# One tanh for each sigmoid, two logarithms for the forget gate, and powers on GpSimd in a two-layer hybrid trunk

## The chip, the core and the metric

The kernel runs on one core of a Trainium2 chip. A core has five engines that each work off a list of their own in order: TensorE (PE: matmuls, with PEld for its weight loads), VectorE (DVE), ScalarE (ACT: one activation function per element with a scale and a bias), GpSimd (POOL) and SyncE (SP: here it issues most of the DMAs). They meet through semaphores. The metric is device time in microseconds (us) of one execution; the time of a kernel is the median over its runs.

## The reference

A trunk of two layers works on x of 256 tokens by 2048 features. What each layer computes, cut to what matters here:

```python
hn = rms_norm(h, norm_w[l])
proj = hn @ w_in[l]                        # 2048 x 8208
# group A, DeltaNet: 8 heads of 128
qkv = silu(causal_conv(dn_qkv, conv_w))
q, k = l2_norm(q) * 128 ** -0.5, l2_norm(k)
beta, g = sigmoid(b), -exp(A_log) * softplus(a + dt_bias)
# group B, HGRN2: 8 heads of 128
q = silu(hg_q)
log_f = log(lb + (1 - lb) * sigmoid(f))    # then summed up over each chunk: G
k = (1 - lb) * sigmoid(-f)
# both: o = recurrence(...); o = rms(o) * norm_w * silu(z)
h = h + concat(y_a, y_b) @ w_out[l]
h = h + (p[l] @ w_ple_up[l]) * sigmoid(h @ w_ple_gate[l])
```

A last rms_norm with final_norm_w ends it. Everything is float32.

## The kernel before

TensorE's fast path for four-byte numbers rounds them, so each matrix is split in two parts, hi (the rounded copy) and lo (the rest), and a product is three matmuls: hi by hi, hi by lo, lo by hi. The weights are read in the order in which they are used, as weight steps of two row tiles of 128 by 512 columns. For each step SP loads `raw` (three buffers, L378), ACT copies it to `whi` (L400), DVE subtracts to `wlo` (L402), and PE does twelve matmuls (L336, in `products`): for each of two token halves and each of two row tiles one with whi, one with wlo, one with whi. A step is prepared up to two steps ahead (`LOOK`), in three buffers of whi and wlo.

Per layer three stages follow one another on PE: in (17 chunks of up to 512 columns of w_in, 16 row tiles each), out (four chunks of w_out) and gate (four chunks of w_ple_gate, with the small product with w_ple_up). The 17 chunks are ordered by hand (`in_order`): the DeltaNet columns k and q of the four groups of two heads, then columns f and q of the HGRN2 groups, mixed with the rest. Whenever a chunk is complete, its mixer starts beside the following chunks: DeltaNet in class `DN`, HGRN2 in class `HG`. A tile named hg11 belongs to HGRN2 in layer 1, group 1; dn03 is DeltaNet in layer 0, group 3. Each mixer is a generator that waits a number of weight steps (tables `DELAY` and `DELAY_AT`) between its parts.

The order of PE is the order of the code: each matmul is kept in program order. On ACT, DVE and POOL a scheduler, which places each instruction by its own estimate of when it can run, writes the order, so that a mixer's operations and the whi and wlo of coming steps are interleaved by that estimate. An engine never goes past an instruction that waits: a wlo that stands behind a gate operation waits for it.

What the change touches, by name:

- `sigmoid` (L461) makes 1/(1 + exp(-x)) from an Exp on ACT, a min and an add on DVE, a Ln and an Exp on ACT. It is used for the convolutions (`conv`), for `gate_z` (SiLU of z, with a product on POOL, L590), in `f_side` and in `q_side`.
- `f_side` of HG (L967 to 979) takes the columns f: e = exp(-f) bounded (L467, L468), sg = the sigmoid (L469 to 471), k = e * (1 - lb) * sg (L974, one instruction for each of the two heads), log f as Ln of (1 - lb) * sg + lb (L975), and G as a running sum over the tokens (L979). `q_side` then makes q (L991) and factors out of G (tiles X, L1012 and following), part by part.
- `after_gate` (L1169) and `Finish.gate` (L1203 to 1208) write the same sigmoid out by hand for the gate stage. `after_gate` serves all chunks but the last one of layer 1, `Finish` that one, in pieces of 256 columns, since nothing runs beside it.
- inverse roots are a Ln and an Exp with scale -0.5 (`rms_factor` L609 and L610; `invn` and `nq` in DN), in `rms_token` and `Finish.rt` with one Newton step behind (L540 to 544).
- `write_gates` (L1139 and following) makes beta and g of DeltaNet, with an Exp and a Ln; the change leaves its code alone.
- ACT holds the tables of a few functions at a time. Before loads one set that has both Exp and Ln, once at the start (L237).

Of the kernel before, what the change touches and what calls it, by code (L numbers as in the profile page):

```python
# [166 lines left out]
def trunk(ctx: ExitStack, tc: tile.TileContext, head, xT, x, pT, W, par, fw, cst, msk, eye, out):  # L167
# [59 lines left out]
    def first_loads():  # L227
# [9 lines left out]
        S.preload_act_table_set("natural_log_exp_and_others")  # L237
# [35 lines left out]
    epsc = cp.tile([128, 1], F32, name="epsc")  # L273
    G.memset(epsc, EPS)
    lnhd = cp.tile([128, 1], F32, name="lnhd")
    G.memset(lnhd, float(-0.5 * np.log(128.0)))
# [31 lines left out]
    oml = cp.tile([128, DEPTH, 8], F32, name="oml")  # L308

    def gate_constants():  # L310

        S.activation(negA, P("alog", 0, DEPTH * 16), AF.Exp)
# [16 lines left out]
        V.tensor_scalar(oml, lb, -1.0, 1.0, ALU.mult, ALU.add)  # L329

# [130 lines left out]
    def sigmoid(dst, src, e=None):  # L461

        if e is None:
            S.activation(dst, src, AF.Exp, scale=-1.0)
            V.tensor_scalar(dst, dst, BIG, 1.0, ALU.min, ALU.add)
        else:
            S.activation(e, src, AF.Exp, scale=-1.0)  # L467
            V.tensor_scalar(e, e, BIG, None, ALU.min)  # L468
            V.tensor_scalar(dst, e, 1.0, None, ALU.add)  # L469
        S.activation(dst, dst, AF.Ln)  # L470
        S.activation(dst, dst, AF.Exp, scale=-1.0)
# [67 lines left out]
    def rsqrt_newton(r, x, t):  # L539
        S.activation(r, x, AF.Ln)  # L540
        S.activation(r, r, AF.Exp, scale=-0.5)
        V.tensor_tensor(t, r, r, ALU.mult)
        V.scalar_tensor_tensor(t, t, -0.5, x, ALU.mult, ALU.mult)
        V.scalar_tensor_tensor(r, t, 1.5, r, ALU.add, ALU.mult)
        return r
# [37 lines left out]
    def gate_z(ps, c0, rt, name):  # L583
# [5 lines left out]
        sigmoid(sz, zs)  # L589
        G.tensor_tensor(sz, zs, sz, ALU.mult)  # L590
# [153 lines left out]
    class DN:  # L744
# [12 lines left out]
        def dz(self, ps, c0):  # L757
            self.sz = gate_z(ps, c0, self.row.rt, self.n)
            self.done.add("z")
            yield 1  # L760
# [24 lines left out]
        def conv(self, ps, which):  # L785
# [11 lines left out]
            sg = tmp(n + "sg")  # L797
            sigmoid(sg, ac)
            return ac, sg

        def conv_silu_kq(self, ps, which, w):
            ac, sg = self.conv(ps, which)
            for t in range(2):
                V.tensor_tensor(self.kq[t][:, :, w, :], v4(ac)[:, t::2], v4(sg)[:, t::2], ALU.mult)
# [24 lines left out]
        def k_side(self):  # L829
# [7 lines left out]
            lk = small("lk")  # L837
            S.activation(lk, ss, AF.Ln, bias=epsc)
            self.invn = small("invn", 4, NG + 1)
            S.activation(self.invn, lk, AF.Exp, scale=0.5)  # L840
# [7 lines left out]
        def q_side(self):  # L848
# [22 lines left out]
            lq = small("lq")  # L871
            S.activation(lq, ss, AF.Ln, bias=epsc)
            self.nq = small("nq", 4, NG + 1)
            S.activation(self.nq, lq, AF.Exp, scale=-0.5, bias=lnhd)
            self.inv.given(self.g)

        def dv(self, ps, c0):
# [3 lines left out]
            ac, sg = self.conv(turned(et, 0, n + "pvc"), 2)  # L881
            V.tensor_tensor(ac, ac, sg, ALU.mult)
# [57 lines left out]
    class HG:  # L940
# [25 lines left out]
        def f_side(self, fs):  # L966
            l, g, n = self.l, self.g, self.n  # L967
            e, sg = tmp(n + "fe"), tmp(n + "fsg")
            sigmoid(sg, fs, e)
            self.k = mix("hk", 512, 1, n + "k")  # L970
            for m in range(2):
                sl = slice(256 * m, 256 * m + 256)
                hd = 2 * g + m
                V.scalar_tensor_tensor(self.k[:, sl], e[:, sl], oml[:, l, hd:hd + 1], sg[:, sl], ALU.mult, ALU.mult)  # L974
# [430 lines left out]
```

## Time and profile before

| what | value |
| --- | --- |
| runs | 1248.42, 1246.96, 1245.05 us |
| median | 1246.96 us |
| span of the profiled execution | 1246.4 us, 0.6 below the median |
| granted TensorE clock, mean | 0.996 |
| matmuls | 8385 |
| weight copies whi on ACT | 392, 1051 ns each, 411.6 us |
| weight differences wlo on DVE | 392, 1234 ns each, 483.0 us |
| first instruction of the tail's chain behind the last matmul | 1236.70 us |

The profile is one execution on the chip, with the start and the length of each instruction. Spans of PE instructions overlap, since matmuls are pipelined: the twelve of a step start 0.227 us apart, 2.72 us in all. A row of the timeline gives the start in us from the span's start, the length in us, the engine, the line of the kernel, the operation, and what it writes from what it reads; several instructions of one kind in a row are one row with their count (x2). In brackets stands idle time ahead of it, with what ended that. A row of waits gives who waits for whom: us in total, how many times, the longest.

### The profile page before, as it was taken

How to read it: one execution, taken by the hardware profiler on the slowest of the kernel's cores; microseconds unless marked ns; L12 is line 12 of the kernel's file. 1: busy time of each engine (PE TensorE's matmuls, PEld its weight loads, DVE VectorE, ACT ScalarE, POOL GpSimd, SP SyncE). 2: the span in 40 equal slices, each digit the busy share in tenths (PEclk: the TensorE clock that was granted, in tenths of full speed). 3: DMA queues.
4: the chain of work that ended last, by engine and by line, in shares of the span. 5: the costliest groups of instructions: out<-in, count | busy, mean ns of one | idle time of the engine just before them, and what ended most of it. 6: DMA issues, size and time to landing. Idle time of an engine off the chain costs nothing.

```text
span 1246.4 us, 21626 instructions
## 1 busy us (share of the span) xinstructions
PE 1229.5 (99%) x8385; PEld 1033.1 (83%) x8385; DVE 880.0 (71%) x1520; ACT 778.1 (62%) x1397; POOL 69.5 (6%) x64
## 2 busy tenths in 40 slices
PE   9999999999999999999999999999999999999996
PEld 7888887798888888888888888887888888888886
DVE  7777796878568656547567778977876695565566
ACT  7676776586757744437556768674766576444464
POOL 0310000000000000000003100000000000000010
PEclk9999999999999999999999999999999999999998
DMA  8555555435464445555555555555445555656563
GB/s 288 174 178 175 174 174 160 170 122 187 152 219 153 170 177 184 187 186 186 187 184 170 174 178 165 177 175 154 134 140 165 172 156 185 207 179 181 183 203 135
DMA packets 73719, 218.71 MB, mean 175 GB/s; under 512 B 15504, under 2 KB 20752, under 8 KB 73616
## 3 DMA queue, kind: packets, MB, share of 16 engines
q1 hardware_dynamic: 63392, 211.78, 52.0%
q10 hardware_dynamic: 10224, 5.54, 1.5%
q8 instruction: 66, 1.08, 0.3%
q14 instruction: 37, 0.30, 0.1%
HBM read 212.84 MB, written 4.46 MB: 174 GB/s over the span
## 4 chain that ended last, share of the span: by engine, by line
PE 89%; DVE 6%; ACT 2%; DMA 1%; issue 1%; SPq 0%; DVEq 0%; ACTq 0%
PE out L336 14%; PE gate L336 14%; PE in1hf L336 7%; PE in0dk L336 7%; PE in0dv L336 6%; PE in1dv L336 6%; PE in1dk L336 6%; PE in1hi L336 6%; PE in0hf L336 5%; PE in0hi L336 4%; DVE wlo L402 2%; PE up L336 2%; PE in1dz L336 1%; PE in0dz L336 1%; ACT whi L400 1%
## 5 line engine op out<-in xcount | busy, mean ns | idle before, releaser
L402 DVE TENSOR_TENSOR wlo<-raw,whi 128x1024 fp32r<-128x1024 f32 (+1 forms) x392 | 483.0, 1234 | 273.9 <-ACT whi L400 272.7
L400 ACT ACTIVATE whi<-raw 128x1024 fp32r<-128x1024 f32 (+1 forms) x392 | 411.6, 1051 | 328.2 <-PE out L336 90.8
L336 PE MATMUL in1hf<-whi,n1hi 128*128 128x512 f32 x128 | 51.0, 398 | 0.9 <-issue 0.9
L336 PE MATMUL in1hi<-whi,n1hi 128*128 128x512 f32 x128 | 51.6, 403 | 0.0
L336 PE MATMUL in1dk<-whi,n1hi 128*128 128x512 f32 x128 | 51.3, 401 | 0.0
L336 PE MATMUL in1hi<-wlo,n1hi 128*128 128x512 f32 x128 | 50.0, 391 | 0.7 <-DVE wlo L402 0.7
L336 PE MATMUL gate<-whi,g0hi 128*128 128x512 f32 x128 | 50.1, 392 | 0.0
L336 PE MATMUL in1dk<-wlo,n1hi 128*128 128x512 f32 x128 | 50.0, 391 | 0.1
L336 PE MATMUL in1hi<-whi,n1lo 128*128 128x512 f32 x128 | 50.0, 391 | 0.0
L336 PE MATMUL in1dk<-whi,n1lo 128*128 128x512 f32 x128 | 50.0, 390 | 0.0
L336 PE MATMUL in1hf<-whi,n1lo 128*128 128x512 f32 x128 | 49.9, 390 | 0.0
L336 PE MATMUL in1hf<-wlo,n1hi 128*128 128x512 f32 x128 | 49.9, 390 | 0.0
L336 PE MATMUL gate<-whi,g0lo 128*128 128x512 f32 x128 | 49.8, 389 | 0.0
L336 PE MATMUL gate<-wlo,g0hi 128*128 128x512 f32 x128 | 49.8, 389 | 0.0
L336 PE MATMUL in1dv<-whi,n1hi 128*128 128x512 f32 (+1 forms) x128 | 48.1, 376 | 0.0
L336 PE MATMUL in1dv<-whi,n1lo 128*128 128x512 f32 (+1 forms) x128 | 46.5, 364 | 0.0
L336 PE MATMUL in1dv<-wlo,n1hi 128*128 128x512 f32 (+1 forms) x128 | 46.5, 363 | 0.0
L336 PE MATMUL gate<-whi,g1hi 128*128 128x512 f32 (+1 forms) x120 | 45.5, 379 | 0.0
L336 PE MATMUL gate<-wlo,g1hi 128*128 128x512 f32 (+1 forms) x120 | 45.4, 379 | 0.0
L336 PE MATMUL gate<-whi,g1lo 128*128 128x512 f32 (+1 forms) x120 | 45.4, 378 | 0.0
L336 PE MATMUL in0hi<-wlo,n0hi 128*128 128x512 f32 x96 | 38.3, 399 | 2.0 <-DVE wlo L402 2.0
L336 PE MATMUL in0hi<-whi,n0hi 128*128 128x512 f32 x96 | 39.3, 410 | 0.0
(1495 smaller groups left out, 3172.8 us busy)
## 6 DMA issues: line engine op xcount, KB each, us to landing
raw<-W SPq DMA_DIRECT2D x384, 512.0 KB, 3.5
raw<-W SPq DMA_DIRECT2D x7, 544.0 KB, 3.7
h<-x SPq DMA_DIRECT2D x4, 512.0 KB, 4.7
xt<-xT SPq DMA_DIRECT2D x3, 512.0 KB, 5.9
out_dram<-h SPq DMA_DIRECT2D x6, 256.0 KB, 2.2
di0d<-di0Bt ACTq DMA_DIRECT2D x4, 256.0 KB, 2.7
di1d<-di1Bt ACTq DMA_DIRECT2D x4, 256.0 KB, 2.3
fw<-fw ACTq DMA_DIRECT2D x2, 512.0 KB, 5.5
```

The lines of the kernel that those rows point to most:

```text
L336: return tc.keep_in_program_order(nc.tensor.matmul(*a, **k))
L400: S.activation(hi[:, sl], raw[:, sl], AF.Copy)
L402: V.tensor_tensor(lo[:, sl], raw[:, sl], hi[:, sl].bitcast(F32), ALU.subtract)
```

## The change

Every sigmoid outside of write_gates and f_side becomes one Tanh, by sigmoid(x) = (1 + tanh(x/2)) / 2. DVE then makes (t + 1) * x in one instruction. The factor of a half goes into numbers that are there anyway: the convolution weights (halved once at the start), the row factor `rth` for z, the lower-bound constant `omlh`, the split of p. The product of gate_z goes from POOL to DVE.

In f_side log f becomes a difference: Ln(1 + lb * e) - Ln(1 + e), with the difference on DVE, and sigmoid becomes exp of minus the second logarithm: k = e * omlh * exp(-l0). The running sum comes ahead of k in the code.

Inverse roots become powers on GpSimd: one add and multiply on DVE, then `pow` with -0.5 (or 0.5) on POOL. The Newton steps go.

The set of functions loaded at the start is now one with Exp and Tanh in place of the one with Exp and Ln. Nothing in the code says where sets are changed; the built program has 21 table loads on ACT where before had one: two in each of the eight f_side, and two around the Ln of write_gates in each layer.

```diff
-        S.preload_act_table_set("natural_log_exp_and_others")
+        S.preload_act_table_set("exp_and_others")
...
+        V.tensor_scalar(P("cw", 0, DEPTH * 96), P("cw", 0, DEPTH * 96), 0.5, None, ALU.mult)
...
-    def sigmoid(dst, src, e=None):
...
+    def power(dst, src, scale, bias, p):
+
+        V.tensor_scalar(dst, src, scale, bias, ALU.mult, ALU.add)
+        G.tensor_tensor(dst, dst, p.to_broadcast(list(dst.shape)), ALU.pow)
...
-        r, x, t = small2("rt"), small2("rtx"), small2("rtt")
-        V.tensor_scalar(x, ss, 1.0 / D, EPS, ALU.mult, ALU.add)
-        return rsqrt_newton(r, x, t)
...
+        r = small2("rt")
+        power(r, ss, 1.0 / D, EPS, mhalf)
...
-        sigmoid(sz, zs)
-        G.tensor_tensor(sz, zs, sz, ALU.mult)
+        S.activation(sz, zs, AF.Tanh)
+        V.scalar_tensor_tensor(sz, sz, 1.0, zs, ALU.add, ALU.mult)
...
-        S.activation(f, ss, AF.Ln, scale=1.0 / 128, bias=epsc)
-        S.activation(f, f, AF.Exp, scale=-0.5)
+        power(f, ss, 1.0 / 128, EPS, mhalf)
...
-            e, sg = tmp(n + "fe"), tmp(n + "fsg")
-            sigmoid(sg, fs, e)
+            e, l0, l1 = tmp(n + "fe"), tmp(n + "fl0"), tmp(n + "fl1")
+            S.activation(e, fs, AF.Exp, scale=-1.0)
+            V.tensor_scalar(e, e, BIG, None, ALU.min)
...
+            S.activation(l0, e, AF.Ln, bias=onec)
+            for sl, hd in heads:
+                S.activation(l1[:, sl], e[:, sl], AF.Ln, scale=lb[:, l, hd], bias=onec)
+            V.tensor_tensor(l1, l1, l0, ALU.subtract)
+            self.G = mix("hG", 512, 1, n + "G")
+            for sl, hd in heads:
+                V.tensor_tensor_scan(self.G[:, sl], keep, l1[:, sl], 0.0, ALU.mult, ALU.add)
             self.k = mix("hk", 512, 1, n + "k")
...
+            S.activation(self.k, l0, AF.Exp, scale=-1.0)
+            for sl, hd in heads:
+                V.scalar_tensor_tensor(self.k[:, sl], e[:, sl], omlh[:, l, hd], self.k[:, sl], ALU.mult, ALU.mult)
...
-            sigmoid(sg, qr)
+            S.activation(th, qr, AF.Tanh, scale=0.5)
...
         def gate(self, *js):
             t = self.t
             for j in js:
-                S.activation(t[:, RUNS[j]], self.ps[j][:, RUNS[j]], AF.Exp, scale=-1.0)
-                V.tensor_scalar(t[:, RUNS[j]], t[:, RUNS[j]], BIG, 1.0, ALU.min, ALU.add)
-            for j in js:
-                S.activation(t[:, RUNS[j]], t[:, RUNS[j]], AF.Ln)
-            for j in js:
-                S.activation(t[:, RUNS[j]], t[:, RUNS[j]], AF.Exp, scale=-1.0)
+                S.activation(t[:, RUNS[j]], self.ps[j][:, RUNS[j]], AF.Tanh, scale=0.5)
...
-            V.tensor_tensor(t, self.up[:, RUNS[j]], t, ALU.mult)
+            V.scalar_tensor_tensor(t, t, 1.0, self.up[:, RUNS[j]], ALU.add, ALU.mult)
...
-            rsqrt_newton(self.r, self.s3[:, 1:2], self.u)
+            G.tensor_tensor(self.r, self.s3[:, 1:2], mhalf, ALU.pow)
```

The order of PE and of SP stays as it is. On ACT, DVE and POOL the scheduler writes another one. Two places matter for what follows. A number behind a name is that of a buffer or a tile; a wlo belongs to the whi and the raw in its row, and the wlo rows follow one another in the order of the weight steps. A running sum (TENSOR_TENSOR_SCAN in the trace) reads SCALAR_TENSOR_TENSOR here, hg11G by name.

On DVE in layer 1, HGRN2 group 1, before, from the wlo of one step to the wlo of the next one (L468 and L469, the two halves of the sigmoid, stand ahead of the piece):

```order
L402 TENSOR_TENSOR wlo_8524<-raw_8439,whi_8523 128x1024
L974 SCALAR_TENSOR_TENSOR hg11k<-hg11fe,oml,hg11fsg 128x256 x2
L991 TENSOR_TENSOR hg11q<-hg11pq,hg11qsg 128x16x32
L979 SCALAR_TENSOR_TENSOR hg11G<-cs,hg11fsg 128x256 x2
L494 SCALAR_TENSOR_TENSOR hg10lo_8515<-hg10yp,pr,hg10hi_8514 128x512
L1052 TENSOR_TENSOR hg11q<-hg11G 128x16x16
L1012 TENSOR_TENSOR hg11X_8539<-hg11G 128x128x2
L1014 TENSOR_TENSOR hg11X_8539<-hg11G 128x128x2
L1054 TENSOR_TENSOR hg11q<-hg11q 128x16x16
L402 TENSOR_TENSOR wlo_8548<-raw_8490,whi_8547 128x1024
```

The same place after; the first row is the wlo of the step ahead of the one that opens the piece above:

```order
L404 TENSOR_TENSOR wlo_8346<-raw_8249,whi_8345 128x1024
L952 TENSOR_SCALAR hg11fe<-hg11fe 128x512
L957 TENSOR_TENSOR hg11fl_8320<-hg11fl_8320,hg11fl_8319 128x512
L964 SCALAR_TENSOR_TENSOR hg11k<-hg11fe,omlh,hg11k 128x256
L960 SCALAR_TENSOR_TENSOR hg11G<-cs,hg11fl_8320 128x256 x2
L964 SCALAR_TENSOR_TENSOR hg11k<-hg11fe,omlh,hg11k 128x256
L1037 TENSOR_TENSOR hg11q<-hg11G 128x16x16
L997 TENSOR_TENSOR hg11X_8392<-hg11G 128x128x2
L976 SCALAR_TENSOR_TENSOR hg11q<-hg11qth,hg11pq 128x16x32
L489 SCALAR_TENSOR_TENSOR hg10lo_8368<-hg10yp,pr,hg10hi_8367 128x512
L1039 TENSOR_TENSOR hg11q<-hg11q 128x16x16
L404 TENSOR_TENSOR wlo_8377<-raw_8294,whi_8376 128x1024
```

The wlo that stood ahead of k, running sum and q, wlo_8524 before, is wlo_8377 after and stands behind them; of the products for X one stays ahead of it. One half of k stands ahead of the running sums.

On ACT at the same place, before:

```order
L467 ACTIVATE hg11fe<-hg11pf 128x512
L464 ACTIVATE hg11qsg<-hg11pq 128x512
L470 ACTIVATE hg11fsg<-hg11fsg 128x512
L400 ACTIVATE whi_8523<-raw_8439 128x1024
L471 ACTIVATE hg11fsg<-hg11fsg 128x512
L470 ACTIVATE hg11qsg<-hg11qsg 128x512
L491 ACTIVATE hg10hi_8514<-hg10yp,pr 128x512
L471 ACTIVATE hg11qsg<-hg11qsg 128x512
L975 ACTIVATE hg11fsg<-hg11fsg,lb,oml 128x256 x2
L400 ACTIVATE whi_8547<-raw_8490 128x1024
```

And after:

```order
L402 ACTIVATE whi_8345<-raw_8249 128x1024
L951 ACTIVATE hg11fe<-hg11pf 128x512
L954 ACT_TABLE_LOAD
L954 ACTIVATE hg11fl_8319<-hg11fe,onec 128x512
L956 ACTIVATE hg11fl_8320<-hg11fe,onec,lb 128x256 x2
L962 ACT_TABLE_LOAD
L962 ACTIVATE hg11k<-hg11fl_8319 128x512
L974 ACTIVATE hg11qth<-hg11pq 128x512
L486 ACTIVATE hg10hi_8367<-hg10yp,pr 128x512
L1038 ACTIVATE hg11q<-hg11q 128x16x16
L402 ACTIVATE whi_8376<-raw_8294 128x1024
```

Two activations of each sigmoid are gone and two table loads are there, the second between the logarithms and the Exp that k needs. The whi that stood among the sigmoid's parts (whi_8523) is whi_8376, behind the Exp of q.

On DVE in layer 0, HGRN2 group 0, before:

```order
L468 TENSOR_SCALAR hg00fe<-hg00fe 128x512
L402 TENSOR_TENSOR wlo_1674<-raw_1558,whi_1673 128x1024
L469 TENSOR_SCALAR hg00fsg<-hg00fe 128x512
L465 TENSOR_SCALAR hg00qsg<-hg00qsg 128x512
L974 SCALAR_TENSOR_TENSOR hg00k<-hg00fe,oml,hg00fsg 128x256 x2
L402 TENSOR_TENSOR wlo_1695<-raw_1607,whi_1694 128x1024
L979 SCALAR_TENSOR_TENSOR hg00G<-cs,hg00fsg 128x256 x2
L991 TENSOR_TENSOR hg00q<-hg00pq,hg00qsg 128x16x32
```

And after:

```order
L952 TENSOR_SCALAR hg00fe<-hg00fe 128x512
L404 TENSOR_TENSOR wlo_1637<-raw_1524,whi_1636 128x1024
L957 TENSOR_TENSOR hg00fl_1611<-hg00fl_1611,hg00fl_1610 128x512
L964 SCALAR_TENSOR_TENSOR hg00k<-hg00fe,omlh,hg00k 128x256
L960 SCALAR_TENSOR_TENSOR hg00G<-cs,hg00fl_1611 128x256 x2
L964 SCALAR_TENSOR_TENSOR hg00k<-hg00fe,omlh,hg00k 128x256
L1037 TENSOR_TENSOR hg00q<-hg00G 128x16x16
L997 TENSOR_TENSOR hg00X_1673<-hg00G 128x128x2
L976 SCALAR_TENSOR_TENSOR hg00q<-hg00qth,hg00pq 128x16x32
L404 TENSOR_TENSOR wlo_1658<-raw_1572,whi_1657 128x1024
```

Here too the second wlo of the piece, wlo_1695 before and wlo_1658 after, has moved from between k and the running sums to behind the product of q.

More of the change, by code (lines that the diff above doesn't have):

```diff
@@ L272, in trunk @@
     keep, ident32 = cs[:, 256:512], cs[:, 512:544]
[L273 to L276, printed above, removed]
+    half, mhalf = (cp.tile([128, 1], F32, name=x) for x in ("half", "mhalf"))
+    G.memset(half, 0.5)
+    G.memset(mhalf, -0.5)
     onec = cp.tile([128, 1], F32, name="onec")
@@ L836, in k_side @@
                             ALU.mult)
-            lk = small("lk")
-            S.activation(lk, ss, AF.Ln, bias=epsc)
             self.invn = small("invn", 4, NG + 1)
-            S.activation(self.invn, lk, AF.Exp, scale=0.5)
+            power(self.invn, ss, 1.0, EPS, half)
             self.b, self.nb = small("b", 4, NG + 1), small("nb")
@@ L870, in q_side @@
             pq, ss = self.stat(1, "ssq")
-            lq = small("lq")
-            S.activation(lq, ss, AF.Ln, bias=epsc)
             self.nq = small("nq", 4, NG + 1)
-            S.activation(self.nq, lq, AF.Exp, scale=-0.5, bias=lnhd)
+            power(self.nq, ss, 128.0, 128.0 * EPS, mhalf)
             self.inv.given(self.g)
@@ L1171, in after_gate @@
         for m in range(2):
[L1172 removed]
+            S.activation(t[m], ps[m], AF.Tanh, scale=0.5)
         for m in range(2):
[L1174 to L1179 removed]
+            V.scalar_tensor_tensor(t[m], t[m], 1.0, up[m], ALU.add, ALU.mult)
             V.tensor_tensor(h[c][:, m], h[c][:, m], t[m], ALU.add)
```

69 lines of the change are left out of this document (22 added, 47 removed).

## The prediction

> **What bounds the kernel now.** I read the page first, then the waits of TensorE, then the timelines of PE, DVE and ACT around each longer wait, then the chain that ended last.
>
> ```profile
> span 1246.4 us, 21626 instructions
> PE 1229.5 (99%) x8385; PEld 1033.1 (83%) x8385; DVE 880.0 (71%) x1520; ACT 778.1 (62%) x1397; POOL 69.5 (6%) x64
> L400 ACT ACTIVATE whi<-raw 128x1024 fp32r<-128x1024 f32 (+1 forms) x392 | 411.6, 1051 | 328.2 <-PE out L336 90.8
> ```
>
> TensorE is busy for 99% of the span; ACT is idle 328.2 us ahead of its weight copies, most of it because no buffer is free until PE has used one. So ACT and DVE work that goes away where they run ahead of PE is worth nothing. The change leaves the matmuls as they are; the time can move only by PE's stalls and by what follows the last matmul. The waits of PE that ACT or DVE cause and that are near the change:
>
> ```profile
> PE in0hi L336 <- DVE wlo L402: 2.0, 1, 2.0
> PE in1hi L336 <- DVE wlo L402: 0.7, 1, 0.7
> ```
>
> Both are one place in each layer: HG group 1 (hg01, hg11), where DVE's gate work stands ahead of the wlo of the weight step that PE needs next.
>
> **Price list.** The rows that price what is new: a table load, a multiply and a fill on POOL.
>
> ```profile
> 2.21 1.28 ACT L237 ACT_TABLE_LOAD   x1 [2.21 <-issue]
> ```
>
> ```profile
> 0.80 0.10 POOL L274 MEMSET epsc<- 128x1 f32 x1 [0.29 <-POOLq L1397]
> 44.56 2.04 POOL L770 TENSOR_TENSOR dn00ug<-cs,gp 128x512 fp32r<-128x512 f32 x2 [14.38 <-DVE gp L1160]
> ```
>
> A table load takes 1.28 us; before has one, after has 21 (two around the Ln of write_gates in each layer, two in each of the eight f_side). No row shows a power on POOL. Its ends are 0.10 (128x1 fill) and 1.02 (128x512 product, half of 2.04); at 128x1 or 128x4 it is nearest to the fill. I take 0.2, and 0.35 with the hand-over.
>
> **hg11, layer 1.** DVE, ACT and PE in before:
>
> ```profile
> 822.64 0.42 DVE L468 TENSOR_SCALAR hg11fe<-hg11fe 128x512 f32<-128x512 f32 x1
> ...
> 826.21 1.23 DVE L402 TENSOR_TENSOR wlo<-raw,whi 128x1024 fp32r<-128x1024 f32 x1
> 827.35 0.88 DVE L974 SCALAR_TENSOR_TENSOR hg11k<-hg11fe,oml,hg11fsg 128x256 f32<-128x256 f32 x2
> ...
> 830.05 0.73 DVE L494 SCALAR_TENSOR_TENSOR hg10lo<-hg10yp,pr,hg10hi 128x512 fp32r<-128x512 f32 x1
> 830.69 0.42 DVE L1052 TENSOR_TENSOR hg11q<-hg11G 128x256 f32<-128x256 f32 x1
> ...
> 831.36 0.42 DVE L1014 TENSOR_TENSOR hg11X<-hg11G 128x256 f32<-128x256 f32 x1
> 831.70 0.42 DVE L1054 TENSOR_TENSOR hg11q<-hg11q 128x256 f32<-128x256 f32 x1
> 832.03 1.22 DVE L402 TENSOR_TENSOR wlo<-raw,whi 128x1024 fp32r<-128x1024 f32 x1
> ```
>
> ```profile
> 821.20 0.58 ACT L467 ACTIVATE hg11fe<-hg11pf 128x512 f32<-128x512 f32 x1
> ...
> 827.87 1.10 ACT L975 ACTIVATE hg11fsg<-hg11fsg,lb,oml 128x256 f32<-128x256 f32 x2 [0.60 <-DVE hg11k L974]
> ```
>
> ```profile
> 829.54 0.39 PE L336 MATMUL in1hi<-whi,n1hi 128*128 128x512 f32 x1
> 829.76 0.39 PE L336 MATMUL in1hi<-wlo,n1hi 128*128 128x512 f32 x1
> ...
> 832.26 0.39 PE L336 MATMUL in1hi<-whi,n1hi 128*128 128x512 f32 x1
> 833.31 0.50 PE L336 MATMUL in1hi<-wlo,n1hi 128*128 128x512 f32 x1 [0.66 <-DVE wlo L402]
> ```
>
> A weight step is 12 matmuls, 829.54 to 832.26: 2.72 us. Before, the wlo that PE wants at 829.76 is ready at 827.44, ahead of the gate work; the next one, behind it, is late by 833.31 - 832.49 = 0.82. After, DVE's order puts the first of the two behind the whole gate work as well. The chain there: min ends at 823.06 as before (the first load is hidden by the min: the Exp loses the norm's two short activations ahead of it and ends near 821.4 instead of 821.8, and 1.28 more is 822.7); Ln l0 and two l1 (0.57 and 1.08, as L467 and the L975 pair) end at 824.7; the second load lies bare on the chain until 826.0; Exp k ends at 826.5. The k Exp holds DVE, because the product with k stands ahead of the scans in DVE's order. Then come k, scans, q, X, hg10lo: the stretch from 827.35 to 832.03 in before, 4.68, less one X product of 0.34 that moves behind the wlo: 4.34, to 830.85. wlo, 1.22: 832.07. PE waits 2.3 us at 829.76. Twelve matmuls on it is at 834.8, by when the next wlo (only 0.34 + 1.22 later, 833.6) is ready. Against 833.31 the loss is 1.5 us.
>
> **hg01, layer 0.** The same code with less lead:
>
> ```profile
> 202.66 0.57 ACT L1114 COPY hg00o<-hg00po 128x512 f32<-128x512 f32 x1
> ```
>
> ```profile
> 817.45 0.59 ACT L1114 COPY hg10o<-hg10po 128x512 f32<-128x512 f32 x1 [0.28 <-PE hg10po L336]
> ```
>
> ```profile
> 213.67 0.39 PE L336 MATMUL in0hi<-wlo,n0hi 128*128 128x512 f32 x1
> ...
> 216.16 0.39 PE L336 MATMUL in0hi<-whi,n0hi 128*128 128x512 f32 x1
> 218.51 0.50 PE L336 MATMUL in0hi<-wlo,n0hi 128*128 128x512 f32 x1 [1.95 <-DVE wlo L402]
> ...
> 219.84 0.63 PE L336 MATMUL in0hi<-whi,n0lo 128*128 128x512 f32 x1
> 220.26 0.63 PE L336 MATMUL in0hi<-whi,n0hi 128*128 128x512 f32 x1
> ```
>
> The copy that starts the chain leads PE's need by 213.67 - 202.66 = 11.0 here and by 829.76 - 817.45 = 12.3 there, so the wait is 2.3 + 1.3 = 3.6: PE goes on at 217.3, and one step later at 220.0 where before was at 218.51: 1.5 us lost. Behind before's wait the matmuls stand 0.42 apart instead of 0.23, from 219.41 to 222.40: eight of them, 1.6 us more. TensorE ran at half clock for a while after a gap of 2.35 us between two starts; after the gap of 1.05 in hg11 it did not. After's gaps are 3.8 in hg01 (halved as before, no change) and 2.5 in hg11, which is beyond 2.35: I take the halving there too, +1.7. Without it the forecast is 1.7 lower.
>
> **hg00 and hg10, a new stall.** Here before has no wait:
>
> ```profile
> 149.34 0.60 ACT L467 ACTIVATE hg00fe<-hg00pf 128x512 f32<-128x512 f32 x1 [0.91 <-PE hg00pf L339]
> 149.74 0.37 ACTq L632 DMA_DIRECT2D di0d<-di0Bt  x1
> ```
>
> ```profile
> 155.14 1.23 DVE L402 TENSOR_TENSOR wlo<-raw,whi 128x1024 fp32r<-128x1024 f32 x1 [0.59 <-ACT whi L400]
> ```
>
> ```profile
> 158.46 0.40 PE L336 MATMUL in0hi<-wlo,n0hi 128*128 128x512 f32 x1
> ```
>
> wlo ends at 156.37, 2.1 us early. After, Exp fe and the DMA issue end at 150.1, load to 151.4, three Ln to 153.1, load to 154.3, Exp k to 154.9. On DVE the wlo now stands behind k, scans, q, X and the q product: 4.34 less hg10lo (0.64) and the last q product (0.33), 3.37, to 158.3; wlo to 159.5. The cover of 2.1 is gone and PE waits 1.0, in each layer: +2.0.
>
> **hg03 and hg13.** By the same count the wlo ends at 389.05 (before: 385.96).
>
> ```profile
> 384.73 1.23 DVE L402 TENSOR_TENSOR wlo<-raw,whi 128x1024 fp32r<-128x1024 f32 x1
> ```
>
> ```profile
> 389.12 0.39 PE L336 MATMUL in0dv<-wlo,n0hi 128*128 128x512 f32 x1
> ```
>
> PE needs it at 389.12: nothing lost, nothing left. hg02 and hg12, counted alike, come out no worse: zero.
>
> **The tail.** After the last matmul, the chain of before:
>
> ```profile
> 1237.11 0.31 DVE pg L1204
> ...
> 1238.34 0.44 DVE pg L1213
> ...
> 1239.78 0.21 ACT fr L540
> ...
> 1240.64 0.17 DVE fr L544
> ...
> 1240.84 1.33 ACT h L1226 x2
> ```
>
> Tanh takes the place of the first Exp; the min, the Ln and the second Exp, 1237.09 to 1238.34, go: 1.25. Ln, Exp and three Newton steps, 1239.78 to 1240.84, 1.06, become one power at 0.35: 0.71. Gain 1.96.
>
> **Costed at nothing.** Where after_gate, the conv, gate_z and q lose two activations each, ACT ran ahead of PE (the 328.2 above); the gate product that goes from POOL to DVE (about the 0.73 of hg10lo, as wide, for a min like the 0.42 above that goes) lies in the same slack, as do the powers in the DN norms and the halved constants, some small DVE instructions. If that cover were missing, each would cost its own 0.2 to 0.7.
>
> **Sum.** -1.96 + 1.5 + 1.5 + 1.7 + 2.0 = +4.7. The span of 1246.4 becomes 1251.1; the median of the runs is 0.6 above this span, so 1251.7.
>
> One page speaks against the change in this very place. The Trainium skill, ScalarE: Activation LUTs, section What ACT_TABLE_LOAD costs, gives a switch about 1283 ns of load plus about 1380 ns of drain, 2.66 us in all. The load agrees with the row of 1.28; whether there is a second part no run here shows, since before's one load has no ACT work ahead of it that could drain. By the page's figure the sum would be some 20 us higher, about 1271 (an estimate).
>
> **Rivals.**
>
> *The loads and the order cost nothing (faster).* The f_side chains fill with the time that ACT saves ahead of them, so that the covers hold. With the second load off the chain (-1.28 in each group) hg00 and hg10 have no stall, hg01 and hg11 lose 0.2 each without a halving: -1.96 + 0.4 = 1244.9 span, 1245.5 median. If in addition the two wlo come before PE's need, the old waits go as well: 2.1 + 1.6 in hg01, 0.8 in hg11, 1239.9 span, 1240.5. It decides from 3.6 us less between hg00's copy and the wlo. For it: the chain loses an Exp and a Newton-free norm ahead of it; ACT stands idle 0.60 at L975 in before. Against it: the order of DVE, in which the wlo is behind Exp k. Chance 0.24, about half of it below 1243.2.
>
> *The switch holds ACT for longer than the load's row.* Suppose that the activations before and after a load stand still for as long again, 2.56 a switch. Then on the chain of hg00 and hg10 2 x 1.28 more, hg01 and hg11 0.96 + 1.28 (the first load gets out of its cover by 823.96 - 823.0), hg03 and hg13 about 2.4 (no slack left), the Ln of write_gates 1.28: 2 x (2.56 + 2.24 + 2.4 + 1.28) = 17, 1268 span. For it: only that no row shows a switch between two activations. Against it: the one row there is, 1.28. Chance 0.07. This is what the page above would give, nearly.
>
> *The power on POOL is slow.* At 2.0 us instead of 0.35 (beyond the 1.02 of the nearest product) the tail gains only 0.3, and hg01 and hg11 wait 1.65 more each, since the power for hg00f stands ahead of yt, and yt ahead of the wlo and the min: +4.95, 1256.6 median. It turns the tail to a loss from 2.3 us on. For it: the only POOL products of before are as slow as 1.02. Against it: they hold 512 elements, the power 1 to 4. Chance 0.11.
>
> **How the numbers follow.** A measurement of this kernel can tell about 0.3%, 3.7 us: the limits are 1243.2 and 1250.7. The forecast has 0.58, of which 0.34 ends above 1250.7 and 0.24 (without the halving in hg11, or a wait shorter by a few tenths in each place) below. Rival one gives 0.14 faster and 0.10 same, rival two 0.07 and rival three 0.11 slower. Faster 0.14, same 0.34, slower 0.52. The range leaves out the lower half of rival one and rival two: 1243.5 to 1257.5.
>
> **What would show it.** Right: PE waits for wlo of 1 us each in in0hi and in1hi at hg00 and hg10, of 3.6 and 2.3 at hg01 and hg11 with a spell at 0.42 between matmuls behind each of these; the second load of each f_side directly ahead of Exp k with DVE idle; a tail whose h products start 2 us sooner behind the last gate activation; POOL powers of 0.1 to 0.4. Wrong: no PE wait for wlo at hg00; loads that take more or that leave a gap behind them; a power over 1 us; or a PE wait at a place not named here, the start of either layer above all, where write_gates now holds two loads.

## The result, and the profile after

The changed kernel takes 1262.14 us (median of 5 runs, 1257.76 to 1263.88) against 1246.96 before: ratio 1.0125, 95% interval 1.0107 to 1.0143. It is slower by 15 us, 10.4 more than forecast and above the range. The profiled execution has a span of 1262.0 us (its own time is 1263.68).

The head of the page of after, busy time by engine:

```profile
PE 1236.5 (98%) x8385; PEld 1037.2 (82%) x8385; DVE 866.1 (69%) x1494; ACT 725.5 (57%) x1213; POOL 91.8 (7%) x84
```

ACT has 53 us less work, DVE 14 us less, and PE, with the same 8385 matmuls, stands still for longer. The waits of TensorE in after (total, times, longest):

```profile
PE in0hi L338 <- DVE wlo L404: 2.4, 2, 1.3
PE in1hi L338 <- DVE wlo L404: 2.4, 2, 1.3
PE dn12yp L341 <- DVE dn12yt L562: 2.1, 1, 2.1
PE in0hi L338 <- ACT whi L402: 1.6, 1, 1.6
PE in1hi L338 <- ACT whi L402: 1.6, 1, 1.6
PE hg11pa L338 <- issue: 1.6, 1, 1.6
PE hg01po L338 <- ACT hg01Ax L1089: 1.6, 1, 1.6
...
PE dn02yp L341 <- DVE dn02yt L562: 1.0, 1, 1.0
```

Before had one row for wlo in each of in0hi and in1hi, 2.0 and 0.7, and of the other rows here only that of hg11pa, 1.0. Since the order of PE is the same in both kernels, the loss can be read place by place: the start of each matmul in after less the start of the same matmul in before, and how much that difference grows from one place to the next. The table gives this growth in us for after and for all experiments, each from its one profiled execution against that of before; "behind it", behind the last matmul, is what the tail adds.

```
place                  after    e1     e2     e3     e4     e5     e11    e12    e7     e8     e9     e10
start of layer 0        0.54   0.07   0.73   0.63   1.92   0.29   0.21   0.14   1.38   1.77   0.23   0.01
hg00                    1.19  -0.05   1.19  -0.07  -0.15  -0.07  -0.13  -0.18  -0.08  -0.13  -0.11  -0.15
hg01                    1.13  -0.98   0.18  -1.56  -2.05  -0.51  -0.71   0.47   0.49  -1.50  -1.69  -1.64
hg01po                  1.77  -0.07   1.77  -0.06  -0.05   1.77   0.54  -0.06  -0.05  -0.05   0.00  -0.03
dn02yp                  1.84   0.87   0.91  -0.03   0.59   0.83   0.85   1.91   0.03   0.09   0.09   0.11
up to layer 1          -0.52  -0.50  -0.52  -0.52   0.13  -0.52  -0.52  -0.51   0.09   0.13  -0.03   0.02
hg10                    1.41  -0.17   1.35  -0.19  -0.09  -0.04  -0.19  -0.17  -0.17  -0.09  -0.11  -0.01
hg11                    4.06   0.45   3.16  -0.42   0.70   1.13   1.02   1.53  -0.01   0.03   0.28   0.19
hg11pa                  0.96   0.65   0.95  -1.03  -1.30  -0.15  -2.46  -1.52   0.10  -1.16  -1.47  -0.75
hg11po                  0.53  -0.02   0.53  -0.05   0.00   0.20  -0.03  -0.05   0.00   0.00   0.00   0.04
dn12yp                  4.23   0.79   1.96  -0.09   0.64   1.15   0.78   3.35   0.05   0.01   0.05   0.07
up to the last matmul   0.01   0.11   0.01   0.01   0.06   0.01   0.01   0.05   0.05   0.01   0.00   0.01
behind it              -1.54  -1.55  -1.92  -1.93   0.21  -1.55  -1.55  -1.55  -1.55  -0.71   0.01  -1.55
span                   15.61  -0.41  10.31  -5.31   0.60   2.56  -2.18   3.41   0.33  -1.59  -2.75  -3.68
```

Of the 15.6, hg00, hg01, hg10, hg11 and the tail, which the forecast named, hold 1.19 + 1.13 + 1.41 + 4.06 - 1.54 = 6.25. The places that it did not name hold 9.4: hg01po and hg11po 2.3, dn02yp and dn12yp 6.1, hg11pa 1.0, the start 0.5, less 0.5 at the layers' border.

Two things limit how finely the table can be read. A column is one execution: that of e7 took 1248.56 us, 2.5 over its median, and e4's column ends at 0.60 though its median is 2.9 us above that of before. And before's own execution has TensorE at half clock from 219.2 to 222.6 us, in hg01, where eight matmuls stand 0.43 us apart instead of 0.23: 1.6 us. After and e7 have such a spell there too, the other ten columns have none, so 1.6 us of what those show as gained at hg01 is the missing spell.

**hg00.** ACT, DVE and PE in after:

```profile
150.73 1.28 ACT L954 ACT_TABLE_LOAD   x1 [0.30 <-DVE dn03QK L849]
152.03 0.72 ACT L954 ACTIVATE hg00fl<-hg00fe,onec 128x512 f32<-128x512 f32 x1
152.65 1.08 ACT L956 ACTIVATE hg00fl<-hg00fe,onec,lb 128x256 f32<-128x256 f32 x2
153.75 1.28 ACT L962 ACT_TABLE_LOAD   x1
155.05 0.63 ACT L962 ACTIVATE hg00k<-hg00fl 128x512 f32<-128x512 f32 x1
```

```profile
155.71 0.48 DVE L964 SCALAR_TENSOR_TENSOR hg00k<-hg00fe,omlh,hg00k 128x256 f32<-128x256 f32 x1 [1.25 <-ACT hg00k L962]
...
158.94 1.22 DVE L404 TENSOR_TENSOR wlo<-raw,whi 128x1024 fp32r<-128x1024 f32 x1
```

```profile
158.64 0.48 PE L338 MATMUL in0hi<-whi,n0hi 128*128 128x512 f32 x1
160.21 0.50 PE L338 MATMUL in0hi<-wlo,n0hi 128*128 128x512 f32 x1 [1.09 <-DVE wlo L404]
```

This is the forecast chain: both loads lie on it, DVE is idle 1.25 us for the Exp of k, the wlo comes behind k, sum, q and X, and PE waits. A load begins 0.02 behind the end of the Ln ahead of it (152.65 + 1.08 = 153.73) and 0.02 after it the next activation begins: it costs 1.30 and nothing beside.

**hg01.** ACT, then PE:

```profile
215.47 0.42 ACT L1038 ACTIVATE hg01q<-hg01q 128x256 f32<-128x256 f32 x1 [1.38 <-DVE hg01q L1037]
215.79 2.94 ACT L402 ACTIVATE whi<-raw 128x1024 fp32r<-128x1024 f32 x3
```

```profile
214.92 0.39 PE L338 MATMUL in0hi<-whi,n0lo 128*128 128x512 f32 x1
216.89 0.50 PE L338 MATMUL in0hi<-whi,n0hi 128*128 128x512 f32 x1 [1.58 <-ACT whi L402]
218.68 0.51 PE L338 MATMUL in0hi<-wlo,n0hi 128*128 128x512 f32 x1 [1.29 <-DVE wlo L404]
...
220.13 0.63 PE L338 MATMUL in0hi<-whi,n0hi 128*128 128x512 f32 x1
220.56 0.63 PE L338 MATMUL in0hi<-wlo,n0hi 128*128 128x512 f32 x1
```

Here whi is late as well as wlo: three whi (one row, x3) stand behind the part of q on ACT (L1038), which waits for DVE. The 0.43 between the last two rows is the half clock. In hg11 the two gaps between starts are the same as here, 1.97 for whi and 1.79 for wlo.

**hg01po.** The copy hg01Ax on ACT, and PE, which needs it:

```profile
267.85 1.28 ACT L962 ACT_TABLE_LOAD   x1
269.15 0.63 ACT L962 ACTIVATE hg02k<-hg02fl 128x512 f32<-128x512 f32 x1
269.68 0.58 ACT L974 ACTIVATE hg02qth<-hg02pq 128x512 f32<-128x512 f32 x1
270.16 0.36 ACT L1089 COPY hg01Ax<-hg01pa 128x256 f32<-128x256 f32 x1
```

```profile
270.58 0.49 PE L338 MATMUL hg01po<-hg01iv,hg01Ax 128*128 128x128 f32 x2 [1.56 <-ACT hg01Ax L1089]
```

The copy that group 1 needs is queued on ACT behind the whole f_side of group 2, loads included.

**dn12yp.** The power on POOL, the product behind it on DVE, and PE:

```profile
1025.26 1.11 POOL L466 TENSOR_TENSOR fo<-fo,mhalf 128x4 f32<-128x4 f32 x1 [55.40 <-DVE fo L465]
```

```profile
1026.40 0.16 DVE L917 TENSOR_TENSOR fo<-fo,nq 128x4 f32<-128x4 f32 x1 [0.90 <-POOL fo L466]
...
1027.49 1.13 DVE L562 SCALAR_TENSOR_TENSOR dn12yt<-dn12o,fo,dn12sz 128x128 f32<-128x128 f32 x4
```

```profile
1027.98 1.17 PE L341 MATMUL dn12yp<-cs,dn12yt 128*128 128x128 f32 x4 [2.13 <-DVE dn12yt L562]
```

DVE stands idle for the power, and dn12yt, for which PE waits, is behind it. The powers by size, from the groups of POOL:

```profile
L466 POOL TENSOR_TENSOR nq<-nq,mhalf 128x4 f32<-128x4 f32 x8 | 16.5, 2060 | 58.1 <-DVE nq L465 58.1
...
L466 POOL TENSOR_TENSOR fo<-fo,mhalf 128x4 f32<-128x4 f32 x8 | 8.3, 1033 | 224.4 <-DVE fo L465 224.4
...
L1198 POOL TENSOR_TENSOR fr<-fs,mhalf 128x1 f32<-128x1 f32 x2 | 1.1, 550 | 19.5 <-DVE fs L1194 19.5
...
L466 POOL TENSOR_TENSOR s0rt<-s0rt,mhalf 128x2 f32<-128x2 f32 x1 | 0.7, 703 | 9.8 <-DVE s0rt L465 9.8
```

Of the 32 powers at 128x4, 28 took 1.01 to 1.12 us; the other four, all of nq, took 1.91, 1.91, 3.25 and 5.39. Why is open; no wait of PE in the list above is for nq.

**The tail.** ACT in after, from the last Tanh to the product that ends the chain:

```profile
1253.85 0.38 ACT L1187 ACTIVATE pg<-gaterun 128x256 f32<-128x256 f32 x1 [2.15 <-PE gaterun L338]
1256.34 1.33 ACT L1205 ACTIVATE h<-h,fr 128x512 f32<-128x512 f32 x2 [2.11 <-POOL fr L1198]
```

2.49 us lie between their starts, where before had 1236.70 to 1240.84, 4.14. Of the 1.65 gained, 1.23 lie ahead of the sum of squares (Tanh for Exp, min, Ln and Exp) and 0.42 behind it: from the sum to the product take 0.67 us with the power, 1.09 with Ln, Exp and Newton.

### The profile page after: what moved, and what is told of

Its sections match the earlier page's. It is cut to its first block, busy times and chain, and to the rows that moved or that the text cites. A ratio compares the mean times of both kernels' runs of the same rounds, so it can differ in the third digit from the quotient of the medians.

```text
span 1262.0 us, 21432 instructions
## 1 busy us (share of the span) xinstructions
PE 1236.5 (98%) x8385; PEld 1037.2 (82%) x8385; DVE 866.1 (69%) x1494; ACT 725.5 (57%) x1213; POOL 91.8 (7%) x84
## 3 DMA queue, kind: packets, MB, share of 16 engines
q8 instruction: 66, 1.08, 0.3%
## 4 chain that ended last, share of the span: by engine, by line
PE 85%; DVE 5%; ACT 5%; issue 3%; DMA 1%; POOL 1%; POOLq 0%; SPq 0%; DVEq 0%; ACTq 0%
PE out L338 14%; PE gate L338 13%; PE in1hf L338 7%; PE in0hf L338 7%; PE in1dk L338 7%; PE in0hi L338 5%; PE in1hi L338 5%; PE in0dk L338 5%; PE in1dv L338 4%; PE in0dv L338 4%; PE up L338 2%; DVE wlo L404 2%; DMA raw<-W 1%; PE in1dz L338 1%; ACT L962 1%
```

## The experiments

Three theories. T: the two table loads of each f_side make the loss. P: the powers do. O: the scheduler's new order does, whatever the gate work costs.

**e1, no loads.** In the changed kernel:

```diff
-            S.activation(l0, e, AF.Ln, bias=onec)
+            S.activation(l0, e, AF.Tanh, bias=onec)
...
-                S.activation(l1[:, sl], e[:, sl], AF.Ln, scale=lb[:, l, hd], bias=onec)
+                S.activation(l1[:, sl], e[:, sl], AF.Tanh, scale=lb[:, l, hd], bias=onec)
...
-        S.activation(ax, ax, AF.Ln)
+        S.activation(ax, ax, AF.Tanh)
```

> The changed kernel with the two logarithms of the f side and the one of the DeltaNet gates written as Tanh, which takes as long and is in the set that is loaded: log f, k and g come out as other numbers, and no table load is left but the first. All else is kept; the scheduler writes its order anew. Theory T (the table loads make the loss: two of 1.28 us lie on the chain from f to the weight differences and hold the copy of hg01Ax behind them) expects the waits at hg00 and hg10 (1.36 and 1.37) to be gone, those at hg01po and hg11po (1.8 and 0.5) too, those of hg01 and hg11 to fall by 1 to 1.4 each, and the second half-clock spell with it: 1262 becomes 1250 to 1254. Theory P (the powers on GpSimd, 1.0 us each at 128x4 in place of a 0.35 that was reckoned, make it) expects the waits at dn02yp and dn12yp (1.9 and 4.3) to stay and no more than 4 us to go: 1258 or more.

1247.93 us, ratio 1.0014 (1.0004 to 1.0025). P as the main cause falls: it allowed no less than 1258. T is right, and its size was too small: not 8 to 12 but 14 us go with the loads. hg00 and hg10 are at zero (table, column e1), hg01po and hg11po too, and of dn02yp and dn12yp 0.97 and 3.44 went as well, which T had not claimed. The wlo at hg00 still stands behind k, sum and q in e1; it is early because the chain from the Exp of f to the end of this wlo is 2.7 us shorter, 0.33 of it an X product that the scheduler put behind the wlo in e1. So O is not the cause by itself; e5 below, where the order at hg00 is kept row for row, is the cleaner test of it.

**e2, no power in the chains.**

```diff
-        power(f, ss, 1.0 / 128, EPS, mhalf)
+        V.tensor_scalar(f, ss, 0.0, 0.1, ALU.mult, ALU.add)
...
-            power(self.nq, ss, 128.0, 128.0 * EPS, mhalf)
+            V.tensor_scalar(self.nq, ss, 0.0, 0.01, ALU.mult, ALU.add)
...
-            G.tensor_tensor(self.r, self.s3[:, 1:2], mhalf, ALU.pow)
+            V.tensor_copy(self.r, self.s3[:, 1:2])
```

> The changed kernel with the powers taken out where they stand ahead of a consumer soon after: the head norms' factors and nq of the DeltaNet queries become constants made by one small DVE instruction, and the last norm's factor is a copy on DVE; the roots are left out. The powers of invn and of the two row factors stay. Theory T expects only the tail's 0.5 us each and little more: 1259 to 1262. Theory P expects the waits at dn02yp and dn12yp (1.9 and 4.3 us) gone, 0.9 less at each of hg01 and hg11, and 0.5 or more in the tail: 1252 to 1255.

1257.11 us, ratio 1.0088 (1.0062 to 1.0113): between the two. The powers cost 5 us of the 15: 0.9 at dn02yp, 2.3 at dn12yp, 0.95 at hg01, 0.9 at hg11, 0.4 in the tail. Not all of it is the power's own time: at dn12yp 1.0 is a shorter wait and 1.3 a half-clock spell that after has and e2 has not, and at hg01 the gap for whi is 0.7 shorter and the spell (1.6) is missing, against 1.3 of new waits behind it. hg00, hg10 and hg01po do not move, as T has it.

**e3, neither** (both edits):

> Both of the above: no table load but the first, and no power in the chains. If T and P together are the cause, what is left is a kernel with fewer ACT activations than before and no new wait: 1241 to 1246. If a third theory, O, holds (the scheduler's new order puts the weight differences behind the whole of the gate work, whatever the gate work costs), waits for wlo at hg00, hg10, hg01 and hg11 stay and it takes 1248 or more.

1242.87 us, ratio 0.9978 (0.9967 to 0.9988). O falls as the main cause: without loads and powers the named places have no new wait, though an X product stands behind the wlo here, as in e1. Loads and powers add up: without the loads 14.2 us go, without the powers 5.0, without both 19.3.

**e4, the kernel before with all inverse roots as powers on GpSimd** (as in the diff of the change; the sigmoids as before):

> The kernel before with one part of the change: all inverse roots as powers on GpSimd (the head norms, invn, nq, the row factors, the last norm), the sigmoids as they were, one table load. Theory T expects no loss: 1246 to 1248, the tail 0.3 to 0.5 us shorter. Theory P expects a loss of 4 us or more, 1251 to 1256, with PE waiting for dn02yt and dn12yt and longer for the wlo at hg01 and hg11.

1249.64 us, ratio 1.0029 (1.0014 to 1.0043). A loss of 3 us, below the 4 of P and above the zero of T. dn02yp, hg11 and dn12yp, the places of P, lose 1.9 together (table). The largest loss in its profile is at another place, the start of layer 0 (1.92). The waits of PE in e4:

```profile
PE in0hi L339 <- DVE wlo L405: 1.4, 1, 1.4
PE in1hi L339 <- DVE wlo L405: 1.4, 1, 1.4
PE dn00pg L339 <- DVE dn00kq L811: 1.3, 1, 1.3
```

dn00pg is new; e10 takes it up. And the tail is no shorter: 0.21 longer. The power itself saves 0.42 there, as in after, but a min of the last sigmoid starts 0.5 later, behind products of the other run on DVE.

**e5, the same loads at another place.** In the changed kernel the first load names the set that has both Ln and Exp, and Exp, load, Ln and Exp are kept in this order; so the Exp of k needs no load, and the second load comes ahead of the Tanh of q. DVE's order from the min to the wlo behind q is the same, row for row, in six of the eight groups (in hg03 and hg13 an X and a q product change places); elsewhere the scheduler moved some rows, and one DMA issue moves behind the Exp of k on ACT.

```diff
-            S.activation(e, fs, AF.Exp, scale=-1.0)
+            pinned(S.activation(e, fs, AF.Exp, scale=-1.0))
+            pinned(S.preload_act_table_set("natural_log_exp_and_others"))
...
-            S.activation(l0, e, AF.Ln, bias=onec)
+            pinned(S.activation(l0, e, AF.Ln, bias=onec))
...
-            S.activation(self.k, l0, AF.Exp, scale=-1.0)
+            pinned(S.activation(self.k, l0, AF.Exp, scale=-1.0))
```

> The changed kernel with as many table loads (21), the powers, and the order of DVE in f_side unchanged; the first load of each f_side names the set that has both Ln and Exp, so that the second load falls behind the Exp of k, ahead of the Tanh of q, instead of ahead of the Exp of k. If what costs is the place of the second load on the chain to k, running sum and wlo, it takes 1.28 us off the waits at hg00, hg10 (1.36 each, so they nearly go) and at hg01, hg11 (1.3 each, the half-clock spell of hg11 with it), and leaves hg01po, hg11po, dn02yp and dn12yp as they are, since ACT is held as long: 1262 becomes 1255 to 1258. If it is the time of ACT in itself that costs, wherever the load stands, nothing moves: 1260 to 1263.

1249.85 us, ratio 1.0030 (1.0019 to 1.0042): 12 us less with the same 21 loads, more than the 4 to 7 that were expected. With the order at hg00 kept, this also tells against O. ACT in e5 at hg00:

```profile
153.12 0.62 ACT L963 ACTIVATE hg00k<-hg00fl 128x512 f32<-128x512 f32 x1
153.75 1.28 ACT L975 ACT_TABLE_LOAD   x1
155.04 0.60 ACT L975 ACTIVATE hg00qth<-hg00pq 128x512 f32<-128x512 f32 x1
```

DVE and PE in e5 at the same place:

```profile
157.08 1.22 DVE L404 TENSOR_TENSOR wlo<-raw,whi 128x1024 fp32r<-128x1024 f32 x1
```

```profile
158.71 0.39 PE L338 MATMUL in0hi<-wlo,n0hi 128*128 128x512 f32 x1
```

The load lies beside DVE's k and running sums; the wlo ends at 158.30, 0.4 ahead of its use. In the table the waits at hg00, hg10 and the half-clock spells of hg01 and hg11 are gone, and of dn12yp 3.1 us, which was expected to stay (1.4 of it is a half-clock spell). hg01po keeps its 1.77, as expected, since ACT is held as long.

**e11, e5 with the copy on DVE:**

```diff
-            S.copy(Ax, v4(pa)[:, 0:2])
+            V.tensor_copy(Ax, v4(pa)[:, 0:2])
```

> e5 (the changed kernel with the second load behind the Exp of k) with the copy hgAx of the HGRN2 groups on DVE in place of ACT. If the waits at hg01po and hg11po are head-of-line waits on ACT, behind the next group's f_side with its two loads, they go: 1.6 to 2.3 us less than e5's 1249.85, so 1247.5 to 1248.3. If the copy waits for something else (its product from PE), they stay: 1249 to 1251.

1246.96 us, ratio 1.0010 (1.0000 to 1.0020), 2.9 less than e5 (2.5 by the ratios) and a little more gained than expected. The wait for hg01Ax is gone; it was a wait in ACT's queue, behind work that the copy does not need. The 0.54 left at hg01po belong to other waits. With all 21 loads this kernel takes what e1 takes with one (ratios 1.0010 and 1.0014): the twenty loads cost nothing that these runs can tell once they are neither on the chain to a weight step nor ahead of what PE waits for.

**e12, the power doubled.** On e1, so without the loads in f_side:

```diff
         power(f, ss, 1.0 / 128, EPS, mhalf)
+        G.tensor_tensor(f, f, onec.to_broadcast(list(f.shape)), ALU.pow)
```

> e1 (no loads but the first; log f, k and g other numbers) with a second power, by one, behind the power of every head norm's factor: 16 more powers at 128x4, about 1.0 us each. If a power on these chains costs as much as it takes, each of dn02yp, dn12yp, hg01 and hg11 shows 0.8 to 1.1 us more and the rest nothing: 1247.9 becomes 1251 to 1252.5. If the cost lies in the number of hand-overs or elsewhere (invn, nq), it stays within 1 us of e1: 1247 to 1249.

1252.13 us, ratio 1.0046 (1.0031 to 1.0060), 4 us over e1, as P has it for these chains. Against e1 the table shows 1.04 at dn02yp, 2.56 at dn12yp, 1.45 at hg01, 1.08 at hg11 and 2.2 given back at hg11pa, where e1 has a half-clock spell and e12 has none. The places are the expected ones; dn12yp has more than the power's own time because a half-clock spell follows the wait there (1017.3 to 1020.7 us) and none does in e1.

**e7, the change in the gate stage alone**, on the kernel before: Tanh in after_gate and Finish, the last norm and the two row factors as powers, one load kept in place behind the last Tanh of layer 0.

> The kernel before with the change in the gate stage alone: Tanh in place of the sigmoid in after_gate and in the last chunk, the last norm's factor and the two row factors as powers on GpSimd; all else, f_side and the norms of the mixers too, as before. The sets change three times where nothing waits (four table loads in all). Only the tail should move, by the 1.5 us that it is shorter in the changed kernel (9.7 to 8.2): 1245 to 1246, ratio 0.9985 to 0.9995. If table loads cost where ACT has slack as well, it is 1247 or more.

1246.03 us, ratio 1.0005 (0.9992 to 1.0017): no gain. The tail is 1.55 shorter, as expected, and the start loses 1.38: PE waits 1.3 us for dn00kq, as in e4.

**e8, e7 and the two logarithms in f_side:**

> As the run above, and f_side with the two logarithms of the change, in the set that has Ln and Exp, so without a load between them. The chain to the wlo in f_side is shorter by one activation and two small DVE instructions: the old waits at hg01 and hg11 (2.0 and 0.7, and the half-clock spell of 1.6 in hg01) should shrink or go, by 1 to 4 us: 1241 to 1245.

1246.48 us, ratio 1.0000 (0.9990 to 1.0010): a miss. The start loses 1.77, the wait for dn00kq again. The 1.50 at hg01 is the half-clock spell that is missing here, and the tail's gain is 0.71 and not 1.55 because the last DMA takes 0.7 us longer behind the last product.

**e9, the two logarithms alone**, on the kernel before:

> The kernel before with f_side of the change alone (two logarithms, their difference, k by an Exp), one table load, no power, no Tanh. If the loss of the changed kernel lies in the loads and the powers, this part alone is no loss: 1243 to 1247. If it lies in the new order of f_side (k, running sum, q and X all ahead of the wlo), it takes 1249 or more, with waits for the wlo at hg00 and hg10.

1245.65 us, ratio 0.9995 (0.9985 to 1.0004): no loss, though the wlo at hg00 stands behind k and the sums here too (the q product and X stand behind it). The logarithms themselves, in one set with Exp, are harmless.

**e10, e8 with the row factors as before** (Ln, Exp, Newton step):

> The kernel with the change in the gate stage and the two logarithms in f_side (e8), but with the row factors made as before, by Ln, Exp and a Newton step. In e8 PE waits 1.3 us for dn00kq near 60 us, which before does not have; if the power of the first row factor is its cause, that wait goes and 1.5 us with it: 1244 to 1245.5, ratio to before 0.998 to 0.999, faster than both kernels. If the wait stays, it comes from another part, and the time is that of e8, 1246 to 1247.

1244.02 us against 1246.03, ratio 0.9982 (0.9973 to 0.9990): 0.2% faster than before. The waits of PE in e10 have no dn00pg:

```profile
PE in0hf L339 <- DVE wlo L405: 1.5, 1, 1.5
PE warm L339 <- DVE zeros L238: 1.1, 1, 1.1
PE hg11pa L339 <- issue: 1.1, 1, 1.1
```

The start is at 0.01 in the table where e8 has 1.77. So the edit of the row factor made that wait. It was not the time of the power: from the first instruction of the row factor to its first reader on DVE e8 takes 0.99 us (39.67 to 40.66), before 2.02 (39.15 to 41.17). What differs is the order that the scheduler wrote behind it. The first copy of dn00kqet on ACT, which feeds dn00kq by way of PE, in before and in e8:

```profile
41.23 0.69 ACT L597 ACTIVATE dn00kqet<-in0dk,s0rt 128x512 f32<-128x512 f32 x1 [1.45 <-DVE s0rt L544]
```

```profile
42.79 0.68 ACT L605 ACTIVATE dn00kqet<-in0dk,s0rt 128x512 f32<-128x512 f32 x1
```

In before it is the first to read the factor on ACT; in e8 it stands behind beta, gax and gate_z's copies, and dn00kq starts 1.05 us later (59.21 against 58.16). In e10 the order is before's again. So at this one place a theory like O fits the rows; no run moves the copy alone.

## Why the prediction was wrong

**What held.** The direction, and the mechanism at the four groups and in the tail. hg00 and hg10: forecast 1.0 each, the table has 1.19 and 1.41. hg01: 1.5, measured 1.13. hg11 with its half clock: 3.2, measured 4.06; the spell came, and without the powers the place shows 3.16 (e2). The waits in hg01 and hg11 were forecast at 3.6 and 2.3 for wlo alone; both are 3.3, half of it for whi, which the forecast's chain did not have. Tail: -1.96, measured -1.54; the Tanh gained the forecast 1.25, the power 0.42 and not 0.71. Together 4.7 was forecast and 6.25 came. The load's 1.28 us was right to the digit. The halving in hg11 was forecast from the gap's length; the last section shows that the length alone does not decide it, so this term was right in part by luck.

**Where it failed, first: the waits were sought at the weight steps alone.** The step "hg03 and hg13 ... nothing lost, nothing left" followed the chain to the wlo and stopped there. The wlo was indeed in time to about a quarter of a us, but the slip of ACT and DVE went on to what they do next, the head norm of DeltaNet group 2, and PE waited for dn02yt and dn12yt: 6.1 us. For hg02 and hg12, taken as zero, it was the copy of hg01Ax and hg11Ax, behind the f_side of the next group on ACT: 2.3 us. e5 and e11 show the first to depend on where the load stands and the second on the copy's queue. The forecast listed all of PE's waits before, but no consumer that had been just in time. The same fault is in "Costed at nothing", where "the powers in the DN norms" lie in ACT's and DVE's slack: at dn02yp and dn12yp there was none, and without the powers (e2) 3.2 of the 6.1 us go.

**Second: the price of the power.** "At 128x1 or 128x4 it is nearest to the fill. I take 0.2, and 0.35 with the hand-over." It is 0.55 at 128x1, 0.70 at 128x2 and, in all but four cases, 1.01 to 1.12 at 128x4. The upper bound (1.02, from the product of 512 columns) was the better row, though the likeness was in the engine and not in the size; it was also the shortest of its kind, since POOL's 38 products of 128x512 in before took 1.04 to 2.27 us each. With the missing cover at the DN norms this is worth 5 us (e2 against after, e3 against e1). The rival of the slow power had the right mechanism, with 2.0 us, but sought it at hg01 and hg11, where e2 finds 0.95 and 0.9 of the 5; the DN norms hold 3.2.

**Third, the start.** The powers of the row factors have no term in the sum. In after itself the start loses only 0.54, but in e4, e7 and e8, which keep the sigmoid of three activations ahead of dn00kq, 1.4 to 1.9, by the order that came with the power (e10). Two of the forecast's signs of being wrong did come, a power over 1 us and PE waits at places that it did not name.

**The rivals.** The one that the switch holds ACT for longer, span 1268, was about as near to the span of 1262.0 as the slow power's 1256, and is wrong as a mechanism: the rows at hg00 show 1.30 from the start of a load to the start of the next activation, with three Ln just ahead of it. The drain of about 1380 ns that the Trainium skill (ScalarE: Activation LUTs, What ACT_TABLE_LOAD costs) adds to each switch does not appear here; the loads' part of the loss, 14 us by e1, is made by what stood behind them. The one that loads and order cost nothing, 1240 to 1245, is what e3 shows for the order once loads and powers are out of the chains, 1242.87.

**What stays open.** dn12yp loses 4.23 where dn02yp, the same code in layer 0, loses 1.84. Of the 2.4 between them, 1.1 is a longer wait (gaps between starts of 2.52 and 1.39) and 1.3 are matmuls at half clock, from 1028.7 to 1032.1 us, which dn02yp does not have. The longer wait goes with a weight DMA that is late there: whi waits 1.64 us for it, a norm's squares are queued behind that whi on ACT, and DVE stands idle 0.85 us for it. Why the DMA is late was not tried.

```profile
1022.62 1.06 ACT L402 ACTIVATE whi<-raw 128x1024 fp32r<-128x1024 f32 x1 [1.64 <-DMA raw<-W]
1023.59 0.39 ACT L913 ACTIVATE junk<-dn12o,nq 128x128 f32<-128x128 f32 x1
```

```profile
1023.71 1.23 DVE L404 TENSOR_TENSOR wlo<-raw,whi 128x1024 fp32r<-128x1024 f32 x1 [0.85 <-ACT whi L402]
```

hg11pa's wait, "issue" in the list, moves between -2.5 and +1.0 from kernel to kernel with no edit at it, so a gain or loss there says little.

## What to carry to other kernels

When work on an engine's queue gets longer, go through everything queued behind it up to the next long pause and ask who waits for each: a weight step has its lead and is easy to see, a small copy or a norm's factor that was just in time has none. A table switch cost its 1.3 us here only where it stood on a chain; name the set that serves the whole stretch, and put the switch behind the last function that the chain needs. Do not price a new kind of instruction by the smallest row there is: a few elements on GpSimd took as long here as its products of 512 columns. And where a scheduler writes the order, a faster instruction can still cost by the order that comes with it, as the row factor did; compare the order behind the edit before costing it at nothing.

## What the runs showed of the hardware

A power on GpSimd took 0.55, 0.70 and mostly 1.01 to 1.12 us for 1, 2 and 4 elements in each of 128 partitions: about 0.4 and 0.15 for each element, an estimate from these three, and at four elements as much as the shortest products of 512 columns (1.04). The first logarithm of f_side, with a column of biases, took 0.72 us at 128x512, where the Exp of k, which reads no such column, took 0.63.

The half clock behind a wait isn't set by the gap alone: a gap of 2.35 us between two starts had it in before, one of 2.56 at the same matmuls in e12 did not. The two rows at e12's gap, and the two behind it, 0.23 apart:

```profile
213.42 0.39 PE L338 MATMUL in0hi<-whi,n0hi 128*128 128x512 f32 x1
215.98 0.50 PE L338 MATMUL in0hi<-wlo,n0hi 128*128 128x512 f32 x1 [2.17 <-DVE wlo L404]
216.32 0.39 PE L338 MATMUL in0hi<-whi,n0lo 128*128 128x512 f32 x1
216.55 0.39 PE L338 MATMUL in0hi<-whi,n0hi 128*128 128x512 f32 x1
```

The records of the granted clock show more. In the thirteen traces (before, after and eleven experiments) ten spells lie ahead of the last matmul, each 3.41 us long at a clock of 0.50, and each starts a whole number of 3.413 us behind the first clock record of its trace (in after at 219.72, 840.94, 861.42 and 1028.68 us: 182, 6 and 49 such pieces apart). In the piece directly ahead of each spell PE stood idle for 1.39 to 2.36 us by the rows of its matmuls; a piece with less idle time was not followed by a spell, and none with more than 1.56 was without one; between 1.39 and 1.56 both occur. Before's gap lies in one piece with 1.95 us idle; a border at 215.17 cuts e12's gap into pieces with 1.35 and 0.82. The first record lies between 4.1 and 7.0 us after the start of the trace and differs from execution to execution, so one and the same wait can bring a spell, some 1.6 us, in one execution and none in another.
